# Unread products and a fixed VectorE order around the two routers of a hybrid mixer and mixture-of-experts kernel

## The chip, the cores and the metric

The kernel runs on one core of one Trainium2 chip. The metric is the device time of one execution in microseconds (us), the median of several runs. One further execution was taken with the hardware profiler; all rows below come from it.

## What is computed

Two layers over 512 latent tokens and 256 context tokens of width 1024. Each layer is a token mixer (a combined projection, a gated convolution, a two-way recurrent scan, an output projection) followed by a mixture of 32 experts, of which every token takes two. The part around the change, cut from the reference:

```python
g_logits = tf @ w_rg + b_rg
g_sel = argmax(g_logits); p_group = softmax(g_logits)[g_sel]
e_logits = (tf @ w_re + b_re)[of the 8 experts of g_sel]
top_p, top_i = top_k(softmax(e_logits), 2)
gate = p_group * top_p / sum(top_p)
...
a, u = split(x_blk @ w_gu[e]); y = (silu(a) * u) @ w_down[e]
out[row_tok] += y * row_gate
```

The first layer routes 768 tokens (6 tiles of 128), the second 512 (4 tiles).

## The kernel before, in words

Work is given to a scheduler that orders each engine's instructions by program order and by when it expects their inputs; an engine inside a `manual_schedule` block keeps the order of the program. TensorE (PE), VectorE (DVE), ScalarE (ACT) and GpSimd (POOL) each work through their own list in that order. DMA of expert weights goes through SyncE's queue (SP), which is held in program order from before the router to the end of the experts (`ms2` in `run`).

Each layer has these stages: `mixer` with `proj_out` at its end, which also makes the router's logits; `route`; the experts (`moe`); and, after the first layer's experts, `combine`, with which the second mixer begins.

`route` is a generator with two parts. **Part one** (up to the first `yield`, from L912) finds each token's group and two experts on VectorE: maxima (`gm`, `m1`, `m2`), their one-hots (`goh`, `oh`), the choice matrices `A` and `C`. TensorE counts tokens per expert with small bf16 products (L936 to L941). From the counts come the positions `pc`, and the tables of the three *static* experts (7, 8 and 9, whose weights are loaded ahead) with `table`, `spread` and `index`: products L987, a copy L967, two products L969, index arithmetic. Then the other experts are ranked by size (L1030 to L1039), which gives their order `eid`, `prefix` and `nov` (L1055, L1056). **Part two** (from L1060) makes the gates: softmax pieces `expo` (two ScalarE calls each, L899, L900), `G`, its bf16 pieces `gp` (L1073 to L1077), the static experts' gates with `gated` (products L1091), the rows' copy L1104, a chain over all choices that ends in `zc` and `blk` (L1115, L1116), one-hots and values for the two large tables, and then these tables (L987 again), their indices (L880, L882) and gates (L1091, L1095), for blocks of 64 and of 32 rows.

Between the two parts, `run` starts the three static experts: for each, POOL gathers its rows (L1189), TensorE transposes them (L1211, into the PSUM tile `pS`, of which there are two), VectorE copies them to SBUF (L1213, `xT`), and TensorE multiplies them by the gate and up weights (`gate_up`, L1230). Their second halves (`end`: `activate`, `down`, L1250 to L1297) come after part two, since the tiles that they need lie where the router's tiles lay. In an fp32 product each call of the kernel is two records of the trace, in a bf16 or fp32r product one.

In the kernel before, VectorE is not held to program order in the routers. In the second mixer's front, which adds the first layer's expert outputs to the stream (`combine`, L1588), normalises it (`square`, `rstd`, `norm_next`) and begins the first projection, it is.

Of the kernel before, what the change touches and what calls it, by code (L numbers as in the profile page):

```python
# [33 lines left out]
class Backbone:  # L34
# [530 lines left out]
    def mixer(self, l, ps, st, ms):  # L565
# [10 lines left out]
        with pool("hy", "right") as hy, pool("wp", "right") as wp, pool("sg", "right") as sgp:  # L576
# [16 lines left out]
            with pool("p0", "right") as p0:  # L593
                if l == 0:
                    XT = self.norm_first(H, p0, ps)
                    ast = {}
                    for k in range(8):
                        self.ada_step(0, 0, k, ast, p0, ps, nc.sync, 3)
                    self.ada_cols(0)
                    W = nat(6)  # L600
                    for i in range(6):
                        self.modulated(0, i, H, lambda k: XT[:, k, 128 * i:128 * i + 128], p0)
                        val(W, i)
                else:
                    W = nat(6, range(2), nc.vector)

                    with tc.manual_schedule(engines={mybir.EngineType.DVE}):
                        sq, pt = {}, {}
                        for i in range(-2, 6):
                            if i == -1:  # L610
                                pt[0] = self.norm_next(sq[0], self.X[:, 0, :], p0, ps)
                            if i + 2 < 6:
                                self.combine(0, i + 2, p0)
                            if i == -2:
                                W += nat(6, range(2, 4), nc.gpsimd)
                            if i == -2 or i == -1:
                                sq[i + 2] = self.square(self.X[:, i + 2, :], p0)
                            if i >= 0:
                                self.modulated(l, i, H, lambda k: pt[i][k // 4][:, 128 * (k % 4):128 * (k % 4) + 128], p0)
                                if i + 1 < 6:  # L620
                                    pt[i + 1] = self.norm_next(sq[i + 1], self.X[:, i + 1, :], p0, ps)
                                if i + 2 < 6:
                                    sq[i + 2] = self.square(self.X[:, i + 2, :], p0)
                                val(W, i)
# [237 lines left out]
    def route(self, l, pool, ps):  # L862
# [8 lines left out]
        def T(shape, dt=F32, p=128):  # L871
            return pool.tile([p] + shape, dt, name=f"r{next(ti)}")
# [37 lines left out]
        g = L[:, :nt, 0:4]  # L910
        gm = T([nt])
        nc.vector.reduce_max(gm, g, axis=AX)  # L912
        goh = first_max(g, 4, gm, T([nt, 4]))
        AP_ = T([2, nt, 32])
        E = AP_[:, 0].rearrange("p t (i g) -> p t i g", g=4)
        tt(E, L[:, :nt, 4:36].rearrange("p t (g i) -> p t i g", g=4),
           goh[:, :, :].unsqueeze(2).to_broadcast([128, nt, 8, 4]), OP.mult)
# [1 line left out]
        nc.vector.reduce_sum(e8, E, axis=AX)  # L919
        m1, m2 = T([nt]), T([nt])  # L920
        nc.vector.reduce_max(m1, e8, axis=AX)
        oh = T([2, nt, 8])
        first_max(e8, 8, m1, oh[:, 0])
        nc.vector.scalar_tensor_tensor(e8, oh[:, 0], -3.0e38, e8, op0=OP.mult, op1=OP.add)
        nc.vector.reduce_max(m2, e8, axis=AX)
        first_max(e8, 8, m2, oh[:, 1])
        A = T([2, nt, 32])
        for c in range(2):
# [14 lines left out]
        bc2 = lambda a: a.unsqueeze(1).to_broadcast([128, 2, nt, 32])  # L943
        ppv = pp[:, :32 * nt].rearrange("p (t e) -> p t e", e=32)
        tt(AP_, A, bc2(ppv), OP.mult)
        pc = T([2, nt])
        nc.vector.reduce_sum(pc, AP_, axis=AX)

# [105 lines left out]
        nc.tensor.matmul(rk[:, 256:289], ovb, self.tri[:32, :33], start=True, stop=True)  # L1054
        nc.vector.tensor_copy(self.prefix, rk[:, 256:289])  # L1055
        nc.vector.tensor_copy(self.nov, rk[:1, 288:289])  # L1056
        yield

        gd = tt(T([nt, 4]), g, bl(gm, 4), OP.subtract)
# [46 lines left out]
        dl = tt(T([32]), self.prefix[:, :32], fl, OP.subtract)  # L1106
        nc.vector.scalar_tensor_tensor(dl, dl, float(NB + 1), base, op0=OP.add, op1=OP.subtract)
        bt = lambda a: a.unsqueeze(1).to_broadcast([128, nt, 32])
        w = tt(AP_[:, 0], pos, bt(room), OP.is_ge)
        tt(w, w, bt(dl), OP.mult)  # L1110
        tt(w, w, bt(base), OP.add)
# [1 line left out]
        tt(A, A, bc2(w), OP.mult)  # L1113
        zc = T([2, nt])
        nc.vector.reduce_sum(zc, A, axis=AX)  # L1115
        nc.vector.scalar_tensor_tensor(blk, zc, -1.0, blk, op0=OP.add, op1=OP.add)  # L1116
        nc.scalar.copy(self.pf[:, :, :, :nt], pf)

        os64 = onehot(A[:, :, :, :].bitcast(BF).rearrange("p c t b -> p (c t) b"), slot)
# [26 lines left out]
        for n, k, f in self.pairs[l]:  # L1146
            for h in range(2):
                pr = slice(64 * h, 64 * h + 64)
                nc.vector.tensor_copy(self.gt128[pr, :, n:n + k], self.gt64[pr, :, f + h:f + h + 2 * k - 1:2])
        yield  # L1150


    def load_chunks(self, e, which, tiles, q=None):
# [420 lines left out]
                    self.merge(64, ps)  # L1574
        self.scats = scats

    def combine(self, l, i, cp):

        nc = self.nc
        y = cp.tile([128, 2, D], F32, name="y", bufs=3)  # L1580
# [5 lines left out]
        x = self.X[:, i, :]  # L1586
        for j in range(2):
            nc.vector.tensor_add(x, x, y[:, j, :])  # L1588

    def finish(self):  # L1590
        tc, nc, io = self.tc, self.nc, self.io
# [53 lines left out]
    def run(self, stop=99):  # L1645
        tc, nc = self.tc, self.nc
        self.plan()
        with ExitStack() as st:
# [12 lines left out]
            for l in range(2):  # L1661
                with ExitStack() as ms:
# [3 lines left out]
                    with ExitStack() as rs:  # L1666
# [9 lines left out]
                        with self.pool("mx", l, "right") as xp:  # L1676
# [15 lines left out]
                            with self.pool("rt", l, "right") as rp, self.pool("xq", l, "right") as xq:  # L1692
# [13 lines left out]
                                else:  # L1706
                                    self.slots = ra[:4] + r1 + r2 + r0[2:] + r3[:1] + ra[4:] + r0[:2] + r3[1:]
                                rt = self.route(l, rp, ps)
                                next(rt)
                                stat = []  # L1710
                                for j, w in enumerate(self.pre):
# [14 lines left out]
                                nc.gpsimd.memset(xw, 0.0)  # L1726
                                self.xbs[0], self.YB = ([xw[:, 0]], [xw[:, 1]]) if l else ([xw[:, 0], xw[:, 1]], [])
                                next(rt)
                            self.dbgout(l, L=self.L, G=self.G, eid=self.eid, nov=self.nov)
                            if stop == 4 * l + 1:  # L1730
                                return
# [34 lines left out]
```

## Time and profile before

| what | us |
|---|---|
| median of 3 runs | 2002.74 (2002.5 to 2003.29) |
| the profiled execution's own time | 1996.57 |
| its span, first to last instruction | 1994.8 |
| first router, from the last logits to the last gate table | 561.5 to 605.9 |
| second router | 1481.4 to 1522.4 |
| end of the first layer's experts to the second mixer's first transpose | 1087.1 to 1100.5 |

Rows of a timeline read: start, duration, engine, line, operation, tile written and tiles read, shapes, number of instructions merged into the row, and in square brackets the idle time of that engine just before, with what ended it. The granted clock is TensorE's: 1.00 is 2.4 GHz and 0.50 is 1.2 GHz.

### The profile page before, as it was taken

How to read it: one execution, taken by the hardware profiler on the slowest of the kernel's cores; microseconds unless marked ns; L12 is line 12 of the kernel's file. 1: busy time of each engine (PE TensorE's matmuls, PEld its weight loads, DVE VectorE, ACT ScalarE, POOL GpSimd, SP SyncE). 2: the span in 40 equal slices, each digit the busy share in tenths (PEclk: the TensorE clock that was granted, in tenths of full speed). 3: DMA queues.
4: the chain of work that ended last, by engine and by line, in shares of the span. 5: the costliest groups of instructions: out<-in, count | busy, mean ns of one | idle time of the engine just before them, and what ended most of it. 6: DMA issues, size and time to landing. Idle time of an engine off the chain costs nothing. (4 is left out here: it accounts for less than half of the span.)

```text
span 1994.8 us, 33498 instructions
## 1 busy us (share of the span) xinstructions
PE 1700.2 (85%) x13488; PEld 1098.2 (55%) x13488; DVE 914.0 (46%) x2141; ACT 458.2 (23%) x897; POOL 394.3 (20%) x308
## 2 busy tenths in 40 slices
PE   5998999999968999888875899898968898888885
PEld 2766778798843444333332688777754344334342
DVE  4425255635664132222322637666563644445444
ACT  3512223323212122122211533333320100110011
POOL 1502212111122111111110632222111211111110
PEclk8999999999988999999987899999987999999998
DMA  7376562263489979999997322114478989999995
GB/s 276 101 271 212 179 212 76 76 242 90 168 326 374 418 317 379 417 416 418 417 419 298 135 82 57 54 43 157 137 280 324 417 342 417 418 417 418 417 418 241
DMA packets 141513, 542.35 MB, mean 272 GB/s; under 512 B 17394, under 2 KB 66720, under 8 KB 85417
## 3 DMA queue, kind: packets, MB, share of 16 engines
q1 hardware_dynamic: 118408, 466.17, 59.1%
q10 hardware_dynamic: 15040, 55.08, 8.0%
q0 software_dynamic: 7904, 18.90, 2.5%
q8 instruction: 108, 1.77, 0.4%
q14 instruction: 53, 0.43, 0.1%
HBM read 530.95 MB, written 15.96 MB: 274 GB/s over the span
## 5 line engine op out<-in xcount | busy, mean ns | idle before, releaser
L1230 PE MATMUL acc<-w,xT 128*32 128x256 f32 (+1 forms) x3360 | 378.4, 454 | 59.1 <-DVE xT L1213 34.6
L1230 PEld LDWEIGHTS acc<-w,xT 128*32 128x32 f32 (+1 forms) x3360 | 135.2, 119 | 260.6 <-issue 159.0
L322 POOL TENSOR_TENSOR hilo<-raw,hilo 128x1024 fp32r<-128x1024 f32 x64 | 157.3, 2463 | 436.4 <-ACT hilo L319 396.7
L333 PE MATMUL acc<-HA,hilo 128*128 128x384 f32 (+1 forms) x960 | 204.7, 355 | 0.0
L333 PE MATMUL acc<-HB,hilo 128*128 128x384 f32 (+1 forms) x960 | 202.4, 353 | 0.0
L333 PEld LDWEIGHTS acc<-HA,hilo 128*128 128x128 f32 x960 | 168.8, 189 | 16.2 <-issue 4.2
L333 PEld LDWEIGHTS acc<-HB,hilo 128*128 128x128 f32 x960 | 171.0, 190 | 9.2 <-issue 0.8
L1250 ACT COPY au<-acc 128x256 f32<-128x256 f32 (+1 forms) x69 | 31.1, 453 | 594.3 <-PE acc L1230 551.9
L345 PE MATMUL acc<-hilo,HA 128*128 128x512 f32 x504 | 131.2, 412 | 12.8 <-POOL HA L283 6.3
L1189 POOL DMA_INDIRECT xb<-h,idx x63 | 65.7, 1043 | 385.7 <-PE pS L1211 357.1
L345 PE MATMUL acc<-hilo,HB 128*128 128x512 f32 x504 | 125.8, 398 | 3.9 <-DVE hilo L322 3.6
L345 PEld LDWEIGHTS acc<-hilo,HA 128*128 128x128 f32 x504 | 97.9, 198 | 41.0 <-POOL HA L283 7.5
L1274 DVE SCALAR_TENSOR_TENSOR au<-w,gt,au 32x256 f32<-32x256 f32 (+2 forms) x102 | 58.6, 577 | 114.1 <-ACT au L1273 111.7
L319 ACT CAST hilo<-raw 128x1024 fp32r<-128x1024 f32 x80 | 83.5, 1049 | 119.1 <-PE acc L345 27.5
L345 PEld LDWEIGHTS acc<-hilo,HB 128*128 128x128 f32 x504 | 94.5, 190 | 29.1 <-DVE hilo L322 4.5
L1295 PE MATMUL acc<-w,hT 128*32 128x256 f32 (+1 forms) x816 | 97.2, 478 | 12.4 <-DVE hT L1258 6.4
L389 DVE TENSOR_TENSOR Q<-Q,Dk 128x256 f32<-128x256 f32 (+1 forms) x144 | 89.6, 651 | 23.7 <-PE pA L464 11.8
L1333 PE MATMUL acc<-w,hT 128*32 128x256 f32 (+1 forms) x896 | 87.4, 440 | 7.3 <-DVE hT L1258 5.2
L1181 POOL DMA_INDIRECT yb<-ys,idx x39 | 39.7, 1019 | 260.9 <-DVE ys L1297 185.3
L384 DVE TENSOR_TENSOR K<-K,Dk 128x768 f32<-128x768 f32 x64 | 72.9, 1139 | 21.5 <-ACT tmp L401 17.9
L1295 PEld LDWEIGHTS acc<-w,hT 128*32 128x32 f32 (+1 forms) x816 | 37.4, 126 | 69.5 <-issue 51.3
L1297 DVE TENSOR_TENSOR ys<-acc,au 128x256 f32<-128x256 f32 (+1 forms) x34 | 18.4, 542 | 124.9 <-PE acc L1295 124.5
(369 smaller groups left out, 2245.5 us busy)
## 6 DMA issues: line engine op xcount, KB each, us to landing
w<-in_w_e_gu SPq DMA_DIRECT2D x242, 1024.0 KB
w<-in_w_e_down SPq DMA_DIRECT2D x121, 1024.0 KB
adaw<-in_w_ada ACTq DMA_DIRECT2D x40, 1024.0 KB
raw<-in_w_in SPq DMA_DIRECT2D x64, 512.0 KB
adaw<-in_w_ada SPq DMA_DIRECT2D x8, 1024.0 KB
raw<-in_w_out SPq DMA_DIRECT2D x16, 512.0 KB
HA<-in_w_e_gu SPq DMA_DIRECT2D x6, 1024.0 KB
h<-SG SPq DMA_DIRECT2D x10, 512.0 KB
```

The source lines that it names most:

```text
L319: nc.scalar.copy(W[:, 0], w)
L322: eng.tensor_sub(W[:, 1], w, W[:, 0].bitcast(F32))
L333: nc.tensor.matmul(o, W[:, wi, k, :], H[k // 4][:, k % 4, hi, t], start=k == 0 and wi == hi, stop=k == 7 and wi == 1)
L345: nc.tensor.matmul(pa, H[k // 4][:, k % 4, hi, t], W[k // 2][:, wi, k % 2, :], start=k == ks[0] and wi == hi, stop=k == ks[-1] and hi == 1)
L384: nc.vector.tensor_tensor(half(Kv, TOK, 0, kn, b), half(Kv, TOK, 0, kn, b), vw(Dv, b, [[2 * b, n], [TOK - b, 2], [0, b]]), op=OP.mult)
L389: nc.vector.tensor_tensor(o, o, vw(Dv, (TOK + b) * d, [[2 * b, qn // (2 * b)], [0, b]]), op=OP.mult)
L1181: st = nc.gpsimd.indirect_dma_start(out=rows, out_offset=bass.IndirectOffsetOnAxis(ap=idx, axis=0), in_=yb, in_offset=None, bounds_check=r ...
L1189: self.nc.gpsimd.indirect_dma_start(out=xb, out_offset=None, in_=rows, in_offset=bass.IndirectOffsetOnAxis(ap=idx, axis=0), bounds_check=r ...
L1230: nc.tensor.matmul(pg[kind * u:kind * u + kind, :w], xT[k], gu[:, k % 2, w * u:w * u + w], start=st, stop=sp)
L1274: nc.vector.scalar_tensor_tensor(ms[pr, :o], self.m5s[pr, 0, c], g0[pr], ms[pr, :o], op0=OP.mult, op1=OP.add)
L1295: nc.tensor.matmul(py[kind * u:kind * u + kind, :w], hT[k], dn[k // 2][:, k % 2, w * u:w * u + w], start=k == 0, stop=k == 3)
L1333: nc.tensor.matmul(py[pr, :w], hT[k], dn[k // 2][:, k % 2, c], start=k == 0, stop=k == 3)
```

## The change

A new function `warm` issues a 128x128 by 128x512 fp32 product into the PSUM tile `ada`, which nothing reads there. Its stationary operand is the identity; its moving operand is one column, spread over 512, of the tile given as `after`, so that it waits for that tile (without one, it is a column of the identity, and the product is pinned behind what was issued to TensorE so far). It is called at seven places of the router's part one with one product, at three of part two with two, at the second mixer's front with seven, after each of the two additions of the first tile's `combine`, and after the first tile's norm factor. Besides, VectorE is put in program order from the start of part one to the end of part two.

```diff
                     with tc.manual_schedule(engines={mybir.EngineType.DVE}):
+                        self.warm(ps, n=7)
...
-                                self.combine(0, i + 2, p0)
+                                self.combine(0, i + 2, p0, ps)
...
+                            if i == -2:
+                                self.warm(ps, sq[0][1][:, 0:1])
...
         nc.vector.reduce_max(gm, g, axis=AX)
+        self.warm(ps, gm[:, 0:1])
         goh = first_max(g, 4, gm, T([nt, 4]))
         AP_ = T([2, nt, 32])
+        self.warm(ps, goh[:, 0, 0:1])
...
         nc.vector.reduce_max(m1, e8, axis=AX)
+        self.warm(ps, m1[:, 0:1])
         oh = T([2, nt, 8])
         first_max(e8, 8, m1, oh[:, 0])
+        self.warm(ps, oh[:, 0, 0, 0:1])
...
         nc.vector.reduce_max(m2, e8, axis=AX)
+        self.warm(ps, m2[:, 0:1])
...
         tt(AP_, A, bc2(ppv), OP.mult)
+        self.warm(ps, AP_[:, 0, 0, 0:1])
...
         nc.vector.tensor_copy(self.nov, rk[:1, 288:289])
+        self.warm(ps, pf[:, 0, 0, 0:1])
         yield
...
+        self.warm(ps, rows[:, 0, 0:1], 2)
         w = tt(AP_[:, 0], pos, bt(room), OP.is_ge)
...
         nc.vector.reduce_sum(zc, A, axis=AX)
+        self.warm(ps, zc[:, 0, 0:1], 2)
         nc.vector.scalar_tensor_tensor(blk, zc, -1.0, blk, op0=OP.add, op1=OP.add)
+        self.warm(ps, pf[:, 0, 0, 0:1], 2)
...
+    def warm(self, ps, after=None, n=1):
+        t = ps.tile([128, 512], F32, name="ada", bufs=1)
+        for _ in range(n):
+            c = self.ident[:, 0:1] if after is None else after
+            o = self.nc.tensor.matmul(t, self.ident, c.to_broadcast([128, 512]), start=True, stop=True)
+            if after is None:
+                self.tc.keep_in_program_order(o)
...
-    def combine(self, l, i, cp):
+    def combine(self, l, i, cp, ps):
...
         for j in range(2):
             nc.vector.tensor_add(x, x, y[:, j, :])
+            if i == 0:
+                self.warm(ps, x[:, 0:1])
...
                                 rt = self.route(l, rp, ps)
+                                ms1 = tc.manual_schedule(engines={mybir.EngineType.DVE})
+                                ms1.__enter__()
                                 next(rt)
...
                                 next(rt)
+                                ms1.__exit__(None, None, None)
```

## Rows read from the trace of the kernel before

**Rows 1.** The page's first line.

```profile
span 1994.8 us, 33498 instructions
```

**Rows 2.** Waits in all, times, longest: TensorE 606 to 830, SyncE's queue 560 to 830.

```profile
PE acc L1230 <- DVE xT L1213: 7.6, 9, 1.5
...
SPq L1162 <- PE acc L1295: 74.4, 15, 23.4
```

**Rows 3.** Timeline of TensorE in the first router.

```profile
570.63 0.93 PE L987 MATMUL pS<-r,r 128*32 128x3 bf16 x24 [2.13 <-DVE r L875]
...
578.82 1.92 PE L1230 MATMUL acc<-w,xT 128*32 128x256 f32 x10
...
587.88 0.50 PE L1211 MATMUL pS<-ident,xb 128*128 128x128 f32 x2
...
593.09 0.93 PE L987 MATMUL pS<-r,r 128*64 128x26 bf16 x24
```

**Rows 4.** Windows: length, busy PE, PEld, DVE, ACT, POOL, granted clock, DMA share, GB/s.

```profile
581.00:582.00 1.00, 1.00 (x16) 0.44 (x13) 0.93 (x7) 0.00 (x0) 0.00 (x0) 0.59 0.27 94
...
600.00:606.00 6.00, 4.43 (x75) 3.96 (x74) 3.76 (x20) 0.44 (x2) 1.56 (x2) 0.50 1.01 407
...
613.00:614.00 1.00, 1.00 (x28) 0.55 (x20) 0.79 (x2) 0.38 (x1) 0.41 (x1) 1.00 0.00 0
...
1517.00:1518.00 1.00, 0.64 (x4) 0.54 (x5) 0.92 (x7) 0.00 (x0) 0.69 (x2) 0.53 0.97 401
...
1522.00:1532.00 10.00, 8.48 (x55) 6.17 (x58) 6.20 (x42) 2.64 (x7) 0.00 (x0) 0.50 0.73 294
```

**Rows 5.** Timeline of VectorE in the first router.

```profile
567.45 0.17 DVE L875 TENSOR_TENSOR G<-r,r 128x6 f32<-128x6 f32 x1
...
568.68 0.17 DVE L1077 CAST r<-r 128x12 bf16<-128x12 f32 x1
...
572.65 0.16 DVE L880 TENSOR_SCALAR gts<-pS 128x3 f32<-128x3 f32 x1 [0.48 <-PE pS L969]
...
573.62 0.49 DVE L875 TENSOR_TENSOR r<-r,r 128x18 bf16<-128x18 bf16 x4
...
581.08 0.23 DVE L1104 COPY r<-pA 128x96 f32<-128x96 f32 x1
...
585.50 1.33 DVE L875 TENSOR_TENSOR r<-r,val 128x234 bf16<-128x234 bf16 x4
...
588.42 0.42 DVE L1213 COPY xT<-pS 128x256 f32<-128x256 f32 x1 [1.59 <-PE pS L1211]
...
605.51 0.41 DVE L875 TENSOR_TENSOR gt<-pS,gt 128x28 f32<-128x28 f32 x2 [0.72 <-PE pS L969]
```

**Rows 6.** Timeline of VectorE in the second router.

```profile
1500.41 0.42 DVE L1213 COPY xT<-pS 128x256 f32<-128x256 f32 x1 [2.91 <-PE pS L1211]
1500.75 0.20 DVE L1053 CAST r<-r 32x128 bf16<-32x128 f32 x1
...
1502.65 0.23 DVE L1104 COPY r<-pA 128x96 f32<-128x96 f32 x1
...
1506.11 0.92 DVE L875 TENSOR_TENSOR r<-r,val 128x136 bf16<-128x136 bf16 x4
...
1509.97 0.42 DVE L1213 COPY xT<-pS 128x256 f32<-128x256 f32 x1 [2.73 <-PE pS L1211]
```

**Rows 7.** Timeline of TensorE in the second router.

```profile
1514.35 0.67 PE L987 MATMUL pS<-r,r 128*64 128x17 bf16 x16
```

**Rows 8.** Timeline of VectorE at the front of the second mixer.

```profile
1094.81 2.54 DVE L1588 TENSOR_TENSOR X<-X,y 128x1024 f32<-128x1024 f32 x2 [4.91 <-DMA y<-yb]
...
1101.38 5.53 DVE L1588 TENSOR_TENSOR X<-X,y 128x1024 f32<-128x1024 f32 x2 [1.07 <-DMA y<-yb]
```

**Rows 9.** Timeline of TensorE: fp32 products of 512 columns, and of 128.

```profile
680.23 3.60 PE L1226 MATMUL acc<-w,xT 128*128 128x512 f32 x8
...
1522.78 3.77 PE L715 MATMUL acc<-m5r,ident 8*128 8x128 f32 x16 [0.54 <-ACT au L1250]
```

## The prediction

> **What bounds the kernel now.** I read the page's first line, then the waits, then the timelines of TensorE and VectorE through the routers, then the granted clock in short windows. The span is 1994.8 us [rows 1]. After a router the experts' weights stream in, and it would be easy to call the rest DMA-bound. The waits say otherwise for the stretch that matters: from 606 to 830 the waits of TensorE are for VectorE and ScalarE, and none of them is for a weight, while SyncE's queue waits 74.4 us in total for expert products to give buffers back [rows 2]. At 613 the DMA stands still with full buffers [rows 4]. So a router that ends later by some microseconds moves everything behind it by as many; the stream cannot catch up, since what it lacks is free buffers.
>
> Inside the first router the reader should see three pieces. VectorE's part one runs to the static experts' indices at 572.65 [rows 5]. Then TensorE multiplies the three static experts, from 578.82; the third one's rows are transposed only at 587.88, behind the products of the other two [rows 3]. Under these products VectorE does nearly the whole arithmetic of part two: the gates' last pieces by 568.85, the rows' copy at 581.08, the last one-hot values by 586.83; only then, at 588.42, comes the copy of the third expert's rows, for which it waited 1.59 us [rows 5]. The large tables start at 593.09, as soon as TensorE is free [rows 3], and the last gates are done at 605.92 [rows 5].
>
> **VectorE in program order.** This is the costly edit. In the program the three copies L1213 stand ahead of all of part two. Whether TensorE still transposes the third expert late is the compiler's choice; I take it that it does, since TensorE's list is unchanged there and the products of the first two experts come earlier in the program. Then VectorE meets the third copy right after part one, waits for TensorE, and everything that used to lie under the products starts at 588.84. What stands behind a waiting copy does wait: in the second router the cast L1053, small work of part one, ran at 1500.75 behind a copy that had waited 2.91 us [rows 6].
>
> What then lies between the third copy and the first large table, in the first router: seventeen dependent small instructions of the gates (from the code) at the spacing that [rows 5] show, seven in a row from 567.45 to 568.68, so 0.205 us from one to the next and 3.5 in all, plus two ScalarE round trips, 0.35 each as an estimate: 4.2. Six products of one-hots and gates, four of which took 0.49: 0.8 [rows 5]. The static gates' table, priced by the static indices' table, from its products at 570.63 [rows 3] to its use at 572.65 [rows 5]: 2.0. From the rows' copy to the last values, 581.08 to 586.83: 5.75 [rows 5]. The one-hot for the small table, about 0.5 as an estimate from the neighbours. In all 13.25; the table may begin 0.4 before the last value. So it starts at 588.84 + 12.85 = 601.7 instead of 593.09: +8.6. The tail behind it, 12.8 us before (593.09 to 605.92), can no longer fill its waits with the other table's work; I add 1.0 (bounds 0 and 2). Together +9.6.
>
> Second router, four tiles: gates 4.0, one-hots 0.6, table 1.7 (scaled by the shorter tiles), 1502.65 to 1507.03 for rows to values, 4.4 [rows 6], 0.4 for the one-hot, 11.1 in all, less 0.4. From the copy's end, 1510.39 [rows 6], that is 1521.1 instead of 1514.35 [rows 7]: +6.7, and +0.9 for the tail: +7.6.
>
> Part one itself costs nothing by the order: what it gives up in filled waits lies under the gathers. The ranking `eid` comes some tenths later, and the loads that need it wait for buffers anyway [rows 2]. No DMA is moved; POOL's next gathers follow the large tables and come later with them, hidden under the static experts' second halves.
>
> **The products that nobody reads.** Eight records of 512 columns took 3.60 [rows 9], 0.45 each at the full clock; a call is two records, so 0.9. At the low clock sixteen records of 128 columns took 3.77 [rows 9], so a call of 512 costs about 1.9. The five ahead of the counts lie in a wait of TensorE and cost nothing; should the counts be ready sooner, they cost at most the rest of one, 0.9. Those of part two lie in the wait that the program order makes. From `zc` to the first table VectorE needs 3.4 us in the first router and about 2.3 in the second (blocks of the spans above), while four calls take 3.6: +0.2 and +1.3 at the full clock (bounds: 0 for both, or 3.8 and 4.9 at the low clock). I take +1.5.
>
> What they may give back: in the first router the clock came up only at 581.8 (0.59 granted in 581 to 582 [rows 4]), 3.0 us after the products began; at half speed these hold 1.5 us of work, and the transposes ahead some 0.3. So a clock that is kept up gives at most 1.8 per router. Whether it is kept: at 1517 the clock fell while TensorE was busy with small products for 0.64 us of that one [rows 4], so being busy is not enough, and between the products put in there are again mostly small ones. By the row nothing need be gained. The Trainium skill ("TensorE: Matmul & The Clock Gate", section "HAM oscillation") puts the fall on idle gaps between bursts, which these products interrupt; by that rule both 1.8 are saved, and the sum below would be 1.8 lower. I take half by the rows alone, since products of full width lie in every stretch: 0.9 per router, -1.8. The second low stretch, behind the tables, gets no product in its last ten microseconds; nothing is taken for it.
>
> **Ahead of the second mixer.** Seven calls, 6.3 us, lie in TensorE's wait before 1096. The second addition of the first tile overwrites what the product after the first one reads, so VectorE now waits for it: +1.0. Behind it wait the square, the norm factor and the next additions; but those begin at 1101.38, when their own data lands [rows 8], and swallow about that much. Until then VectorE, not TensorE, sets this front, so a warmer TensorE gains little. I take +0.4 (bounds -1.0 and +1.5).
>
> **The sum.** 9.6 + 7.6 + 1.5 - 1.8 + 0.4 = +17.3. It is made against the profiled execution's 1996.57 (1.8 more than its span), so 2013.9 there; the median of the runs is 2002.74, 6.2 above it, and I add the same 17.3: **2020.0 us**. The bounds of this case: each chain 1.5 less, no added tail (-1.9), no product in the way (-1.5), the clock kept (-1.8), a mixer gain (-1.4) make +7.7; each chain 1.5 more, longer tails (+2.1), and half of the low-clock delay (+3.5) make +26. That is 2010 to 2029, most of it below 2026.
>
> **Rivals.** *TensorE takes the third expert's transposes first* (the faster side). Its place is TensorE's order before 588: if L1211 of the third expert stands ahead of the first two experts' products, its copy waits for nothing, part two lies under 14 us of products as before, and the first term of each router falls away. Then the clock decides: the low stretches hold 4.43 us of TensorE's work in 600 to 606 and 8.48 in 1522 to 1532 [rows 4], half of which a full clock would give back, with the 1.8 twice about 10 in all. Against tails of +1.9 and products of +1.5 that leaves 6.7 at most, some 6: about 1997. For it: nothing in the data makes the transposes wait for the products. Against it: the order of before [rows 3], where the products of the first two experts came first.
>
> *The order costs nothing, and the products return nothing*: the transposes go first, the clock still falls among the small products as it did at 1517 [rows 4]. Then +1.9 for the tails, +0.4, less up to 1.8: about 2003. That would also be the outcome if the compiler put the products elsewhere than in the waits, some in front of real ones.
>
> **How the numbers follow.** Forecast 0.66, transposes first and the clock kept 0.22, nothing on balance 0.12. A measurement of this kernel tells about 0.2%, 4 us, from no change. Faster by more is the second case almost alone: 0.22. Within: the third, 0.12. Slower: 0.66. The likeliest case alone has 2010 to 2029; to hold eight in ten the range must take in the third case and the upper part of the second, and at the top it may leave out the rare end: 1995 to 2026.
>
> **What would show it.** Right: in the changed profile VectorE waits some 8 us for the third L1213 of each router, L1104 and the one-hots lie behind it, TensorE's wait before the 64-row L987 grows by 8 and 6 us with unread products in it, and the still stretch of the DMA after the router is longer. Clock: 1.00 where the static products begin would show a kept clock, 0.50 a lost one. Wrong: the third L1211 ahead of the first L1230; or part two's copies still at 581; or a last gate table no later than 606.

## The result, and the profile after

The median went from 2003.01 us (2002.5 to 2007.54, 4 runs) to 2034.03 us (2032.09 to 2036.28, 4 runs). The ratio is 1.0159, with a 95% interval of 1.0136 to 1.0181: the change makes the kernel some 32 us slower. Forecast were 2020.0 and 1995 to 2026. The side was right; the size was not, and the range did not hold the time.

The changed kernel's lines lie 3 to 22 further down: the static experts' transposes, copies and products (L1211, L1213, L1230) are L1233, L1235 and L1252, the tables L987 and L991 are L996 and L1000, the gates' products L1091 are L1101, the rows' copy L1104 is L1114, `combine` is L1610. An unread product is L1170, tile `ada`, two records for a call. First the page's first line, which answers to [rows 1].

```profile
span 2030.3 us, 33654 instructions
```

The timeline of VectorE in the first router, which answers to [rows 5]:

```profile
583.74 0.18 DVE L883 TENSOR_SCALAR eid<-pA 1x32 int32<-1x32 f32 x1 [1.90 <-PE pA L1048]
...
585.49 0.19 DVE L1064 COPY prefix<-pA 128x33 f32<-128x33 f32 x1 [0.30 <-PE pA L1063]
...
585.67 0.73 DVE L1235 COPY xT<-pS 128x256 f32<-128x256 f32 x2
594.99 0.42 DVE L1235 COPY xT<-pS 128x256 f32<-128x256 f32 x1 [8.59 <-PE pS L1233]
...
599.42 1.68 DVE L1087 CAST r<-r 128x12 bf16<-128x12 f32 x1
599.50 1.90 DVE L878 TENSOR_TENSOR r<-r,r 128x18 bf16<-128x18 bf16 x6
602.40 0.15 DVE L976 COPY spr<-pS 32x3 f32<-32x3 f32 x1 [1.00 <-PE pS L1101]
...
603.50 0.25 DVE L1114 COPY r<-pA 128x96 f32<-128x96 f32 x1
...
608.63 1.34 DVE L878 TENSOR_TENSOR r<-r,val 128x234 bf16<-128x234 bf16 x4
613.55 0.20 DVE L976 COPY spr<-pS 64x52 f32<-64x52 f32 x1 [3.58 <-PE pS L1000]
```

The third copy stands at 594.99 with 8.59 us of waiting before it, and L1114 with all its one-hots and values comes behind, at 603.50; before, it ran at 581.08, under the static products. This is the wait that was forecast. Two things were not: the whole ranking, down to `prefix` (585.49), now comes ahead of the first two copies, where before it ended behind them; and at 613.55 VectorE waits 3.58 us more, for the table. The ranking's end in the kernel before:

```profile
578.93 0.42 DVE L1213 COPY xT<-pS 128x256 f32<-128x256 f32 x1 [0.83 <-PE pS L1211]
...
580.91 0.19 DVE L1055 COPY prefix<-pA 128x33 f32<-128x33 f32 x1 [1.25 <-PE pA L1054]
```

What held the table in the changed kernel shows on TensorE (answers to [rows 3]):

```profile
586.12 2.36 PE L1252 MATMUL acc<-w,xT 128*32 128x256 f32 x20 [0.67 <-DVE xT L1235]
...
594.45 0.50 PE L1233 MATMUL pS<-ident,xb 128*128 128x128 f32 x2
...
601.18 1.19 PE L1101 MATMUL pS<-r,r 128*32 128x3 bf16 x36 [2.05 <-DVE r L878]
...
603.81 8.65 PE L1170 MATMUL ada<-r,ident 128*128 128x512 f32 x12 [0.62 <-DVE r L1114]
612.39 0.93 PE L996 MATMUL pS<-r,r 128*64 128x26 bf16 x24
```

The last one-hot value is written at 608.63 + 1.34 = 609.97; the table starts at 612.39, because the six unread calls (twelve records) take from 603.81 to 612.46. The windows say why they take 8.65 us and not the 5.4 of six calls at the full clock (columns as in [rows 4]):

```profile
578.00:580.00 2.00, 0.84 (x1) 0.50 (x2) 1.59 (x10) 0.00 (x0) 1.38 (x2) 0.63 0.02 8
...
603.80:605.00 1.20, 1.19 (x2) 0.68 (x3) 1.10 (x5) 0.00 (x0) 0.00 (x0) 0.50 1.05 437
...
609.00:610.00 1.00, 1.00 (x3) 0.19 (x2) 0.97 (x4) 0.00 (x0) 0.00 (x0) 0.88 1.01 418
...
618.00:628.00 10.00, 5.74 (x79) 4.95 (x80) 5.19 (x26) 0.69 (x2) 2.80 (x3) 0.50 0.46 140
```

They begin at a granted clock of 0.50 (1.2 GHz), after TensorE's short waits, and only in 609 to 610 does it rise. The records themselves are the work during which the clock comes up, and real products wait behind them. In the tail, from 618 on, the clock is at 0.50 again. The first window belongs to part one: there the clock, which had stood at 1.00 since 565, fell (0.63 granted in 578 to 580) while TensorE waited for VectorE.

In the second router the third copy waits as well (VectorE):

```profile
1532.41 0.42 DVE L1235 COPY xT<-pS 128x256 f32<-128x256 f32 x1 [9.79 <-PE pS L1233]
```

Two more places appear there. First, three calls stand among the counting products of part one (TensorE; before, the counts went from 1488.53 to 1489.26 in one piece):

```profile
1508.01 0.20 PE L944 MATMUL pA<-r,onesb 128*128 128x32 bf16 x2
1508.06 1.11 PE L1170 MATMUL ada<-r,ident 128*128 128x512 f32 x2
...
1509.23 1.13 PE L1170 MATMUL ada<-r,ident 128*128 128x512 f32 x2
1510.20 0.25 PE L947 MATMUL pA<-r,onesb 128*128 128x32 bf16 x4
...
1510.48 1.13 PE L1170 MATMUL ada<-r,ident 128*128 128x512 f32 x2
1511.54 0.23 PE L949 MATMUL pA<-onesb,r 128*32 128x1 bf16 x3
```

Second, two of the six calls of part two stand inside the 64-row table, behind its first product (TensorE, then one window):

```profile
1540.10 5.62 PE L1170 MATMUL ada<-r,ident 128*128 128x512 f32 x8 [0.42 <-DVE r L1114]
1545.65 0.20 PE L996 MATMUL pS<-r,r 128*64 128x17 bf16 x1
1545.78 1.99 PE L1170 MATMUL ada<-r,ident 128*128 128x512 f32 x4
1547.69 0.64 PE L996 MATMUL pS<-r,r 128*64 128x17 bf16 x15
```

```profile
1541.00:1542.00 1.00, 1.00 (x3) 0.30 (x1) 0.90 (x5) 0.00 (x0) 0.00 (x0) 0.54 1.07 442
```

Here the calls begin at the full clock, and it falls to 0.50 in 1541 to 1542 while they run, with TensorE busy for the whole of that microsecond.

What comes after a router moves by as much as the router ends later, as forecast: from the second router's last gates to the end of the program it is 473.3 us, before 472.5. The queue of the weights waits longer for buffers, and does not catch up (74.4 us before [rows 2]; SyncE's queue from 580 to 850):

```profile
SPq L1184 <- PE acc L1317: 91.5, 16, 39.3
```

The front of the second mixer, on VectorE:

```profile
1115.84 1.23 DVE L1610 TENSOR_TENSOR X<-X,y 128x1024 f32<-128x1024 f32 x1 [4.92 <-DMA y<-yb]
1118.70 1.23 DVE L1610 TENSOR_TENSOR X<-X,y 128x1024 f32<-128x1024 f32 x1 [1.63 <-PE ada L1170]
...
1122.70 2.83 DVE L306 TENSOR_SCALAR xn<-X,rs 128x1024 f32<-128x1024 f32 x1 [1.35 <-POOL rs L249]
1125.46 2.47 DVE L1610 TENSOR_TENSOR X<-X,y 128x1024 f32<-128x1024 f32 x2
```

The second addition waits 1.63 us for the product that reads what it overwrites (1.0 was forecast). The norm L306 then takes 2.83. The next two additions take 2.47 where they took 5.53 [rows 8], so most comes back: from the first to the last addition 34.0 us, before 33.1.

### The profile page after: what moved, and what is told of

Same layout as the page of the kernel before. It is cut to its first block, busy times and chain, and to the rows that moved or that the text cites. A ratio compares the mean times of both kernels' runs of the same rounds, so it can differ in the third digit from the quotient of the medians.

```text
span 2030.3 us, 33654 instructions
## 1 busy us (share of the span) xinstructions
PE 1748.9 (86%) x13560; PEld 1114.2 (55%) x13560; DVE 918.0 (45%) x2141; ACT 458.0 (23%) x897; POOL 391.4 (19%) x308
## 5 line engine op out<-in xcount | busy, mean ns | idle before, releaser
L1252 PE MATMUL acc<-w,xT 128*32 128x256 f32 (+1 forms) x3360 | 378.0, 458 | 60.3 <-DVE xT L1235 36.0
L1252 PEld LDWEIGHTS acc<-w,xT 128*32 128x32 f32 (+1 forms) x3360 | 135.8, 121 | 263.0 <-issue 167.1
L1211 POOL DMA_INDIRECT xb<-h,idx x63 | 65.5, 1039 | 412.5 <-PE pS L1233 359.6
L345 PEld LDWEIGHTS acc<-hilo,HB 128*128 128x128 f32 x504 | 94.2, 190 | 29.6 <-DVE hilo L322 4.5
L1235 DVE COPY xT<-pS 128x256 f32<-128x256 f32 (+1 forms) x79 | 42.2, 538 | 76.3 <-PE pS L1233 62.6
```

The lines of the kernel that those rows point to most:

```text
L345: nc.tensor.matmul(pa, H[k // 4][:, k % 4, hi, t], W[k // 2][:, wi, k % 2, :], start=k == ks[0] and wi == hi, stop=k == ks[-1] and hi == 1)
L1211: self.nc.gpsimd.indirect_dma_start(out=xb, out_offset=None, in_=rows, in_offset=bass.IndirectOffsetOnAxis(ap=idx, axis=0), bounds_check=r ...
L1235: nc.vector.tensor_copy(t[:, :n].rearrange("p a b -> p (a b)"), pt[:, :128 * n])
L1252: nc.tensor.matmul(pg[kind * u:kind * u + kind, :w], xT[k], gu[:, k % 2, w * u:w * u + w], start=st, stop=sp)
```

## The experiments

The theories. **Order** (A in the first two texts below): the program order of VectorE costs most, by the third copy and what stands behind it. **Products** (B there): the unread products cost most, since they run at the low clock in front of real ones. "+21.6" and the like is the ratio of a kernel's time to that of the kernel before, less one, times 2003 us. As runs of one kernel spread over some 10 us, stretches of the profiled executions are used beside the times. The table has, for each router, three stretches: part one, from the last logits' copy to the first static product; the chain, from there to the first product of the 64-row table; and the tail, from there to the last row that writes gates (starts of rows, all of them). Then come the mixer's front, from the first addition to the end of the last; the sum of the seven less before's; and the difference by the ratio with its 95% interval. In the experiments' rows the line numbers shift by the edits; the tile names stay. The edits shown are cuts, against the changed kernel or against the experiment that is named.

| kernel | first router: part one, chain, tail | second router: the same | front | sum | by the ratio |
|---|---|---|---|---|---|
| before | 17.28, 14.27, 12.42 | 18.89, 14.04, 7.92 | 33.13 | | |
| changed | 20.08, 26.27, 15.20 | 19.62, 23.31, 11.37 | 34.02 | +31.9 | +31.8 (27.2 to 36.3) |
| order_alone | 20.00, 23.18, 16.61 | 17.83, 20.91, 10.40 | 33.10 | +24.1 | +21.6 (17.4 to 25.6) |
| products_alone | 17.58, 16.43, 16.46 | 21.92, 17.10, 11.55 | 33.84 | +16.9 | +13.6 (9.2 to 18.0) |
| order_third_first | 20.77, 19.80, 16.69 | 18.66, 17.51, 10.41 | 33.14 | +19.0 | +16.6 (12.6 to 20.6) |
| gates_later | 20.73, 11.77, 18.53 | 18.33, 11.88, 11.92 | 33.14 | +8.4 | +8.4 (4.4 to 12.4) |
| order_part_one | 17.82, 15.27, 13.36 | 16.52, 13.93, 8.86 | 33.11 | +0.9 | +0.8 (-2.8 to 4.4) |
| tail_free | 20.02, 23.67, 14.78 | 17.76, 21.75, 9.98 | 33.14 | +23.2 | +21.2 (15.6 to 26.6) |
| no_part_two_products | 20.09, 23.68, 16.61 | 19.47, 21.90, 11.00 | 33.80 | +28.6 | +29.6 (24.6 to 34.7) |
| mixer_alone | 17.37, 15.44, 13.37 | 17.82, 14.79, 8.38 | 33.82 | +3.0 | +2.8 (-0.6 to 6.2) |
| mended | 20.75, 13.14, 15.56 | 18.37, 12.06, 10.07 | 33.24 | +5.2 | +4.4 (2.0 to 6.6) |
| mended_products | 20.72, 15.05, 19.59 | 20.25, 14.53, 14.63 | 33.81 | +20.6 | +20.4 (15.8 to 25.0) |
| narrow_products | 20.16, 23.45, 16.62 | 18.49, 21.01, 10.72 | 33.87 | +26.4 | +25.0 (20.6 to 29.6) |
| mixer_no_read | 17.37, 15.40, 13.35 | 18.49, 14.20, 8.39 | 33.23 | +2.5 | +1.2 (-1.4 to 3.8) |

The seven stretches carry the whole difference: sum and ratio agree within 3.3 us in every row. How good the base is, mixer_alone and mixer_no_read tell, whose routers are those of before. The profiled execution of before lay 6.2 us below its median, and its first router is 2.2 and 2.1 us shorter than theirs, 1.1 of it in the chain and 0.9 in the tail; its second router has the shorter tail by 0.5, and part one differs among the three by 1.1 (18.89, 17.82, 18.49). So differences of one us against before are within what one and the same program shows.

**order_alone**: the `ms1` block stays, every call of `warm` goes.

```diff
-        self.warm(ps, gm[:, 0:1])
...
-        self.warm(ps, rows[:, 0, 0:1], 2)
```

> Program order of VectorE through the routers, without any of the unread products. Theory A (the order costs most): the third static expert's copy holds part two back, so the two chains of the prediction come, 9.6 + 7.6 = +17.2 over before, and up to 3 more for part one, which the changed kernel's trace shows some 2 to 3 us late: 2017 to 2024. Theory B (the unread products cost most, because they run at the low clock in front of real ones): the order is worth less than 9 of the 31 us, 2012 at most.

+21.6, at the upper edge of theory Order's range, and two thirds of the change. But the terms differ from the forecast. The chains are +8.9 and +6.9 (forecast 8.6 and 6.7), the tails +4.2 and +2.5 (forecast 1.0 and 0.9), and part one +2.7 and -1.1 (forecast 0; the -1.1 is no gain, since mixer_alone, with the routers of before, has the same 17.82). Part one of the first router, on TensorE and then on VectorE:

```profile
582.97 0.67 PE L1220 MATMUL pS<-ident,xb 128*128 128x128 f32 x2 [0.58 <-DMA xb<-h,idxs]
583.57 0.18 PE L1036 MATMUL pA<-r,pcolb 32*1 32x32 bf16 x1
...
586.37 1.94 PE L1239 MATMUL acc<-w,xT 128*32 128x256 f32 x16 [0.67 <-DVE xT L1222]
```

```profile
583.98 0.18 DVE L880 TENSOR_SCALAR eid<-pA 1x32 int32<-1x32 f32 x1 [3.17 <-PE pA L1039]
...
585.91 0.73 DVE L1222 COPY xT<-pS 128x256 f32<-128x256 f32 x2
```

The ranking's second half stands on TensorE behind transposes that wait for the gathers, and in program order the copies of these very transposes stand behind the ranking on VectorE. Each queue holds up what the other needs: the second pair of transposes ends at 583.64, and the copies start at 585.91. No unread product has a part in it, as this kernel has none.

**products_alone**: all products, `ms1` out.

```diff
-                                ms1 = tc.manual_schedule(engines={mybir.EngineType.DVE})
-                                ms1.__enter__()
...
-                                ms1.__exit__(None, None, None)
```

> All unread products, VectorE scheduled freely as in before. Theory A: part two lies under the static products again; of the unread ones some stand among the products of the first large table (four calls there), 0.9 us each at the full clock and up to 1.9 at the low one, in two routers, so +4 to +14: 2006 to 2016. Theory B: they cost most of the 31 us whatever the order: 2020 or more.

+13.6, at the upper end of theory Order's +4 to +14. Four calls stand between the products of the first large table, as expected; three calls among the counts of the second router ran at the low clock, 2.0 each. Order (+21.6) and products (+13.6) add up to 35.2, against 31.8 for both; that under the order some of the products fall into waits would explain it, but with intervals of some 4 us each the difference is not shown.

**order_third_first**: all three gathers, transposes and copies ahead of the first static products.

```diff
+                                xTs = [self.rows_in(32, self.idxs[:, 0, j:j + 1], self.rows_tile(32), xp, ps) for j in range(len(self.pre))]
```

> Program order of VectorE, no unread products, and the rows of all three static experts gathered, transposed and copied before the first expert's products, so that no copy waits behind products. Theory A1 (the third copy is the one wait that holds part two): part two goes back under the static products, and the time is 10 us or more below the kernel with the order alone: 2003 to 2010. Theory A2 (in program order VectorE meets a second wait right behind it: the static gates' table, whose products TensorE takes after all static products, and the rows' copy with everything to the last one-hot values stands behind that): only the gates' arithmetic is hidden, 1 to 4 us per router, so 2 to 8 us below the order alone: 2012 to 2019.

The time is 5.0 below the order alone by the ratios (some 6 us uncertain), and each chain is 3.4 shorter, so theory A2. VectorE's third copy no longer waits for products, but something else does:

```profile
586.96 0.42 DVE L1222 COPY xT<-pS 128x256 f32<-128x256 f32 x1 [0.48 <-PE pS L1220]
...
600.19 0.15 DVE L967 COPY spr<-pS 32x3 f32<-32x3 f32 x1 [8.11 <-PE pS L1091]
...
601.08 0.25 DVE L1104 COPY r<-pA 128x96 f32<-128x96 f32 x1
```

The wait has only moved: 8.11 us for the static gates' table, whose products TensorE takes behind all static ones, with the rows' copy right behind it in the program.

**gates_later**: as order_third_first, and the static gates' table between the two large ones.

```diff
-        gated(oss, hit, 0, ns, self.gts)
...
+        gated(oss, hit, 0, ns, self.gts, bigs)
         tab = table(os32, ob, ov, n32, NB - n32)
```

> As the one before (program order, no unread products, third expert's rows first), and the static gates' table moved from ahead of the rows' copy to between the two large tables. Theory A1: no difference to the one before beyond 3 us. Theory A2: now nothing of part two ahead of the first large table waits for TensorE, so the table starts when the static products end: another 8 to 14 us less, 2000 to 2008, about the time of before.

Another -8.2, so A2. The time of 2013.1 is 5 above its range; the moved table lengthens the tails by 1.8 and 1.5, which is a part of it. The first large table starts as soon as the static products end:

```profile
596.14 1.04 PE L1239 MATMUL acc<-xw,xT 128*32 128x256 f32 x16
597.11 0.93 PE L987 MATMUL pS<-r,r 128*64 128x26 bf16 x24
```

So two waits, one behind the other, held part two. With the first one gone, the second kept 8.2 of the 13.2 us; the first without the second was not run.

**order_part_one**: program order ends with part one; no products.

```diff
                                 next(rt)
+                                ms1.__exit__(None, None, None)
                                 stat = []
```

> VectorE in program order through part one of each router only, scheduled freely from the first resumption on; no unread products. Theory A (the order's cost sits in what stands behind the third copy and in the tail, and part one costs what the trace of the order alone shows: the static products 2.7 us later than the logits in the first router, 1.1 us earlier in the second): +1.6 over before, 2001 to 2008. Rival (part one alone makes everything late, since the ranking and the rows' copies come 7 us later in the first router): +7 or more, 2010 or more.

+0.8, not to be told from nothing. Theory A's place for the cost holds; freed behind part one, VectorE takes the copies ahead of the rest of the ranking, and part one of the first router loses 0.5 and not 2.7.

**tail_free**: the order, given up ahead of the first large table.

```diff
+        yield
         tab = table(os64, ob, ov, 0, n64)
```

> The order alone, but given up ahead of the first large table, so that VectorE may fill its waits in the tail again; no unread products. Theory A (the tails are longer, 4.2 and 2.5 us by the trace of the order alone, because VectorE no longer prepares the next table's gates while it waits): 5 to 8 us below the order alone, 2017 to 2020. Rival (the tails are longer because TensorE's clock is lower, 0.77 against 0.86 granted from 540 to 660): at most 1.5 us below the order alone, 2023 or more.

The expectation of theory A missed: the time is that of the order alone (-0.4), and the tails give back 1.8 and 0.4 of 4.2 and 2.5. Of what is left, some 1 and 0.5 lie in the base, whose tails were that much shorter than those of mixer_alone; the rest goes with the clock. The windows of the first tail, in tail_free and then in the kernel before:

```profile
613.00:629.00 16.00, 9.04 (x142) 8.05 (x141) 10.16 (x59) 0.77 (x2) 4.98 (x5) 0.50 0.60 207
```

```profile
593.00:606.00 13.00, 7.65 (x143) 6.77 (x142) 9.04 (x56) 0.44 (x2) 6.79 (x6) 0.73 1.01 414
```

Before, the tail follows the static products and begins at the full clock. In the order it follows some 10 us in which TensorE mostly waits, and runs at 0.50 throughout. The other kernels bear this out: with the same program order in the tail, it takes 16.61, 16.61 and 16.62 us in order_alone, no_part_two_products and narrow_products, at 0.50 all the way, and 15.20 in the changed kernel, where the clock stands at 1.00 until 616.

**no_part_two_products**: the changed kernel without the six calls of part two.

```diff
-        self.warm(ps, rows[:, 0, 0:1], 2)
...
-        self.warm(ps, zc[:, 0, 0:1], 2)
...
-        self.warm(ps, pf[:, 0, 0, 0:1], 2)
```

> The changed kernel without the six unread products of part two of each router; those of part one and of the second mixer, and the order, stay. Theory A (they stand in front of the first large table at the low clock, 2.4 us beyond the last value in the first router and 2.4 in the second): 4 to 7 us below the changed kernel, 2027 to 2030. Rival (they pay for themselves by the clock that they hold up in the tables behind them): no less than the changed kernel, 2033 or more.

In time this is inconclusive: -2.2 against the changed kernel, with some 7 us of uncertainty. By the stretches both theories have a part. The table comes 2.6 and 1.4 earlier; the first tail is 1.4 longer, since these products do lift its clock, and the second 0.4 shorter. The net is -1.2 and -1.8.

**mixer_alone**: only the products ahead of the second mixer.

```diff
-                                ms1.__enter__()
...
-        self.warm(ps, gm[:, 0:1])
...
                         self.warm(ps, n=7)
```

> Only the unread products ahead of the second mixer; the routers as before. By the prediction VectorE and the loads set this front: +0.4, with bounds -1.0 and +1.5, so 2001 to 2005. Rival (TensorE's clock sets it, and the products keep it up): 2 to 4 us less, 1999 to 2001.

+2.8 (-0.6 to 6.2), the front +0.7 by the table: the front lies within the forecast's bounds, and there is no gain.

**mixer_no_read**: the same without the two calls in `combine`.

```diff
-            if i == 0:
-                self.warm(ps, x[:, 0:1])
```

> Only the unread products ahead of the second mixer, without the two that read the first tile's rows between its additions. Theory A (the second addition waits for the product that reads what it overwrites, and the norm behind it is caught by a slow moment of VectorE): from the first addition to the first transposes of the mixer 5.7 us as before, where the changed kernel takes 9.7. Rival (the seven products ahead of it delay the transposes on TensorE): 7 us or more stay. In time both are within 4 us of before.

From the first addition to the first transposes it is 6.6 us (before 5.7, changed 9.7, mixer_alone 9.6), and the front is 33.23, before 33.13. That is mostly A. The one us that stays is the product that reads the norm factor: it runs at the low clock, 2.07 us, and the transposes stand behind it, though the norm is done at 1110.51. TensorE, then VectorE:

```profile
1109.78 2.07 PE L1160 MATMUL ada<-rs,ident 128*128 128x512 f32 x2 [5.15 <-POOL rs L249]
1111.65 1.81 PE L309 MATMUL pS<-ident,xn 128*128 128x128 f32 x8
```

```profile
1105.01 2.54 DVE L1600 TENSOR_TENSOR X<-X,y 128x1024 f32<-128x1024 f32 x2 [5.04 <-DMA y<-yb]
...
1109.76 0.75 DVE L306 TENSOR_SCALAR xn<-X,rs 128x1024 f32<-128x1024 f32 x1 [0.76 <-POOL rs L249]
1111.42 5.67 DVE L1600 TENSOR_TENSOR X<-X,y 128x1024 f32<-128x1024 f32 x2 [0.90 <-DMA y<-yb]
```

**mended**: order_third_first, gates_later and tail_free in one, no products.

```diff
+                                xTs = [self.rows_in(32, self.idxs[:, 0, j:j + 1], self.rows_tile(32), xp, ps) for j in range(len(self.pre))]
...
+        yield
         tab = table(os64, ob, ov, 0, n64)
...
+        gated(oss, hit, 0, ns, self.gts, bigs)
         tab = table(os32, ob, ov, n32, NB - n32)
```

> Program order with its found costs taken away one by one: the third expert's rows first, the static gates' table between the large ones, and the order given up ahead of the first large table; no unread products. Theory A (the order's +22 is made of the third copy, the static gates' table, the tail and part one, and nothing else): only part one's 2.5 and a little of the tail stay, 2003 to 2010, and from the logits to the last gates of the first router at most 48 us, where before has 43.97 and the order alone 59.79. Rival (the order has a further cost that these do not touch): 2012 or more.

+4.4 (2.0 to 6.6): theory A in time; the first router takes 49.45 us in all, 1.5 over the 48 that A allowed. Of the order's +21.6 some 17 are explained by these three places. Nothing is gained against before, which had part two under the products anyway.

**mended_products**: the same with all products of the change.

```diff
+        self.warm(ps, rows[:, 0, 0:1], 2)
...
+        self.warm(ps, zc[:, 0, 0:1], 2)
```

> The same with all unread products of the change. Theory A (a product that nobody reads costs its own length wherever TensorE has real work queued behind it): six calls stand among the large table's products of each router now and five ahead of the counts, 8 to 16 us above the kernel without them. Rival (they give back by the clock what they take): within 4 us of it.

+16.0 over mended, the upper end of theory A: with part two hidden no wait is left for the products, and they cost their length and a longer tail.

**narrow_products**: the changed kernel with the products in 16 bits.

```diff
-            c = self.ident[:, 0:1] if after is None else after
-            o = self.nc.tensor.matmul(t, self.ident, c.to_broadcast([128, 512]), start=True, stop=True)
+            c = self.onesb[:, 0:1] if after is None else after.bitcast(BF)[:, 1:2]
+            o = self.nc.tensor.matmul(t, self.onesb, c.to_broadcast([128, 512]), start=True, stop=True)
```

> The changed kernel with each unread product in 16 bits: the same places and waits, one record of 512 columns for two. Theory A (the products cost by their length): in the trace the first large table starts 2 us or more earlier against the last one-hot value in each router, and the counts to indices of the second router are 1 us or more shorter; 3 to 6 us below the changed kernel, 2028 to 2031. Rival (their length does not matter, since they hold up a clock that pays for it): the changed kernel's time or more, 2033 or more.

-6.8 against the changed kernel (some 6 us uncertain), theory A. In the first router the products end ahead of the last value, and the table waits for VectorE alone:

```profile
606.42 1.01 PE L1170 MATMUL ada<-r,onesb 128*128 128x512 bf16 x2 [0.61 <-DVE r L1114]
609.23 2.10 PE L1170 MATMUL ada<-r,onesb 128*128 128x512 bf16 x4 [1.79 <-DVE r L1126]
611.70 0.18 PE L996 MATMUL pS<-r,r 128*64 128x26 bf16 x1 [0.38 <-DVE r L878]
```

From the third copy to the table it is 13.88 us in the first router and 12.03 in the second, where the changed kernel takes 17.40 and 13.24 (in the second router the gain is 1.2 only for the table's first product, and 3.2 for the other fifteen, which no longer stand behind two calls). From the second router's counts to the static indices it is 4.03 for 6.91, and 4.05 in order_alone. So products of half the length cost next to nothing in these places.

## Why the prediction was right and wrong

The sum of the forecast was +17.3, that of the stretches is +31.9. Of the 14.6 between them, 7.7 are the products, 4.8 the tails, 1.6 part one, and 0.5 the chains.

**Right: the program order exposes part two.** The third copy waits 8.59 and 9.79 us behind the first two experts' products, `L1104` and the one-hots lie behind it, and the order alone is slower. The two chains are +8.9 and +6.9 for the forecast's 8.6 and 6.7, but that they agree so closely is in part luck. From the copy's end to the table order_alone takes 13.52 and 11.35 us, where 12.85 and 10.7 were added up; and 1.3 and 1.1 of these are of another origin, slow casts (1.69 us for 0.17 in the first router, 0.96 and 0.68 in the second; see the last section). Without them the pieces were priced some 0.5 too long. And the first chain of before was 1.1 shorter than in other executions of that router; against those the difference is +7.8.

**Incomplete: what the third copy blocks.** "Then VectorE meets the third copy right after part one ... and everything that used to lie under the products starts at 588.84" is so in kind, yet the copy is only the first of two waits. The rival in which TensorE takes the third transposes first was priced at 1997 and given 0.22, because part two would then lie under the products. order_third_first is that case without the products, and took +16.6. The static gates' table was counted as a term of 2.0 in the chain, and that it is itself a wait for the end of all static products was missed.

**Wrong: the tail.** "I add 1.0 (bounds 0 and 2)" per tail, for VectorE's unfilled waits alone; they came out at +4.2 and +2.5 in order_alone. tail_free gives 1.8 and 0.4 of it back, which is that term, and within its bounds of 0 and 2; some 1 and 0.5 lie in the base. The rest goes with the clock of 0.50 in a tail that no longer follows full-width products, which the forecast did not count.

**Wrong: "Part one itself costs nothing by the order: ... it lies under the gathers."** It cost +2.7 in the first router: the end of the ranking took its place ahead of the copies, and `eid` came not "some tenths" but 4.2 us later after the logits (17.6 us for 13.4). In the second router nothing is shown.

**Wrong: the products**, the largest miss. The forecast had +1.5 in front of the tables, -1.8 for the clock and +0.4 ahead of the mixer, together +0.1. Changed against order_alone, the stretches give 31.9 - 24.1 = +7.8, and the ratios +10.2. Of the 7.8, 3.1 and 2.4 lie in the chains, in front of the tables (forecast 0.2 and 1.3): the products were priced at the full clock, but those of the first router run at 0.50 for their first 5 us, and in the second the clock falls 1.0 us after they begin. Another 1.0 is in the second tail, where two calls stand inside the table for 1.99 us. 1.8 lie in the second router's part one ("cost nothing ... at most the rest of one, 0.9"), where three whole calls stand among the counts; from the counts to the static indices it is 2.9 more than in order_alone. 0.9 are ahead of the mixer, and the first tail gives 1.4 back.

The gain of the clock under the static products did not come. From the first of them to the end of the last it is 13.0 us in the changed kernel and 13.4 in order_alone, and in both they begin at 0.50; the full clock comes 2.6 us after their start in the changed kernel, where it took 3.0 before. The products of part one did hold the clock at 1.00, from 565 to 578 in the first router, where before it stood at 0.50 from 565 on; but the work there waits for VectorE, and the clock fell again before the static products began. The Trainium skill ("TensorE: Matmul & The Clock Gate", section "HAM oscillation") puts the fall on idle gaps between bursts. The fall in 578 to 580 agrees in kind, since it lies in a wait of 2.05 us for VectorE that no product filled. The fall in 1541 to 1542 lies in no gap: TensorE was busy throughout that microsecond, and its last wait of more than 1 us had ended at 1538.18. The forecast's half of 1.8 took such waits for filled.

**The range** ended at 2026, and its own case at 2029, because "half of the low-clock delay" was taken for the upper end and 2 us for a tail. The bounds of 3.8 and 4.9 for the products in front of the tables, in the text, did hold the 3.1 and 2.4; the tail's bound of 2 did not hold, and part one had none.

## What to carry to other kernels

A product put in to keep the clock up may itself be the work that runs at the low clock, and whatever is queued behind it on TensorE waits. In these runs it was free where it ended within the wait that it filled, as the 16-bit ones did, and cost its length where real products stood ready behind it. Program order on one engine turns every copy that depends on another engine's late work into a gate for all that follows in the text: look for all such waits in a row, since here moving the first one only showed the second. And a chain that moves out from under full-width products can lose twice, its cover and the clock of what comes after it.

## What the runs showed that was not expected

Small VectorE casts took many times their length where a GpSimd instruction ran beside them. In the changed kernel the cast at 599.42 (1.68 us; its neighbours take 0.17) lies beside this row of GpSimd, and ends with it:

```profile
599.27 1.80 POOL L1752 MEMSET xw<- 128x2048 f32 x1 [16.43 <-issue]
```

The other runs settle it nearly as an experiment would. In the five kernels in which this fill starts just before the cast (changed, order_alone, tail_free, no_part_two_products, narrow_products) the cast takes 1.68 or 1.69 us; in the other nine the two lie apart, and it takes 0.15 to 0.17. In the second router of the same five, two casts take 0.96 and 0.68 beside two fills of tile `X` (from 1536.22 to 1538.08 in the changed kernel), while a subtraction of two SBUF tiles between them keeps its 0.17. The mixer's norm at 1122.70 (2.83 us, 0.75 in mixer_no_read) lies beside a GpSimd operation of 2.33 us from 1122.65, and the additions of the second tile (5.67 us for two in mixer_no_read, 2.47 in the changed kernel) beside the same work in the other case. The Trainium skill ("SBUF — State Buffer", section "Who interferes with whom") names one port pair that these two engines share under an exclusive lock. These rows agree: the same cast is slow beside the fill and quick without it.

What also came as a surprise is how far equal executions differ: from the last addition of the mixer's front to the second router's logits, which no edit touches, it took 350.0 us in order_alone and 359.5 in tail_free. That is why single times could not settle the smaller questions here; the stretches could, down to about one us.
